# A hybrid decoder block on one core: the mixers' front with double pages, early key lengths, an early fetch of the first solved block, and the solver's steps over two blocks

## The chip, the cores and the metric

One core of a Trainium2 chip runs the whole layer as one program. The metric is the device time of that core in microseconds (us), the median of several runs. TensorE is called PE (its weight loads PEld), VectorE DVE, ScalarE ACT, GpSimd POOL and the queue that issues nearly all DMAs SP.

## What is computed

512 tokens of width 1024 go through one layer: a norm, one input projection of 3328 columns whose columns feed two mixers side by side (differential attention with partial rotary, and an RWKV-7 time mix), an output projection, an expert-retrieval FFN, a gated embedding and a final norm. Only the mixers' front is touched. What matters of it:

```python
def rwkv7_mix(z_rw, mu, ...):
    zs = z_rw + (prev - z_rw) * mu          # prev: the row before
    r, k, v, xw, xa, xg = split(zs)
    w = -softplus(-(w0 + tanh(xw) @ w_up)) - 0.5
    a = sigmoid(a0 + xa @ a_up)
    kk = k * k_k;  k = k * (1.0 + (a - 1.0) * k_a)
    kk = kk / max(sqrt(sum(kk * kk per head)), 1e-12)
    # scan over the tokens, per head of 64:
    state = state * d + (state @ -kk) x (kk * a) + v x k;  y = state @ r
```

The attention side turns the first 16 of each 64 columns of q and k by a rotary angle.

## The kernel before, in words

Tokens are worked in four blocks of 128 (NB = 4). Everything is float32; a projection is three matmuls of split halves ("whi" from ACT, L130; "wlo", the rest, from DVE, L141), its weights fetched by SP in pieces of 512 KB into three buffers.

**Order.** In the mixers (`mixers`, L866 on) the order of each engine's instructions and the slots of the buffers are set by a planner at build time, which goes roughly by program order and waits where no slot is free; a few edges written by hand (`behind`) put an instruction after another one on its engine. Working buffers are pages of two sizes: `p2` (32 pages of 512 floats a partition) and `p4` (12 pages of 1024).

**The projections of the time mix.** Four groups of columns, k, l (256 columns), r and v, are projected one after the other for all four blocks (`shift_group`, L423). `consume` scales an accumulator into a page "z"; `shift` loads the rows before it by DMA into a second page "zp" and POOL makes zs = z + (zp - z) * mu in three steps (L448, L449, L451), into a third page for k, r and v.

**Preparations.** Then block by block `rw_prepare` (L470) runs in eight parts, each ended by a yield; after each of them the loop at the end of `mixers` (L942 to L951) takes steps of two other generators: `PACE[b]` steps of the solver and `WEAVE[1 + b][i]` steps of `projections` (the three projections of attention, with rotary and transposes in `da_prepare`, L764). `rw_keys` (L455) is called at the start of a block: kk = k * k_k (L459, DVE), its square (L461, ACT), the sum per head (L463, DVE), a reciprocal square root of 12 small DVE operations (`rsqrt`, L87 on), a clamp (L465), and the scaling (L467). The first part of `rw_prepare` makes sw (L491) and aa (L495) by sigmoids, a running sum of sw by matmul (pcum, L498) and four exponentials; the next two are DVE products of 128x512 (L514 to L533); then 16 transposes (ptr, L545), `diagonal` for ab and ak (L587, L591), four stores of ab to DRAM ("ad", L561), and 256 small matmuls (pg, L570).

**Solver.** `rw_solve(half)` (L595) inverts the triangular 32x32 matrices of two blocks at once: it loads both blocks' ad (sol_u, L607), then 31 steps of a product (L613) and a sum (L615) on DVE that grow with the step, then two stores to "td" (L620). Half 0 runs in the preparation of block 2 (PACE 4), half 1 after the last preparation.

**Solved blocks.** `rw_solved(b)` (L622) clears tt on POOL (L626), loads it from td in four DMAs of 128-byte pieces (L632), loads xg (L634), bhr (L636), ykr, bk and uv (L644), multiplies tt by xg (pwu, L651), evicts to wu (L652) and multiplies wu by bhr (pmt, L663). `rw_states` and `rw_out` follow; attention blocks (`da_block`) and a small projection (`ple_proj`) are mixed in.

SP executes its DMA issues in order: one that waits for an earlier transfer's landing holds all that stand behind it.

Of the kernel before, what the change touches and what calls it, by code (L numbers as in the profile page):

```python
# [8 lines left out]
F32 = mybir.dt.float32  # L9
F32R = mybir.dt.float32r  # L10
# [20 lines left out]

WEAVE = (0, (1, 1, 1, 1, 1, 1, 0, 0), (1, 1, 1, 1, 1, 1, 0, 0), (1, 1, 1, 1, 1, 1, 0, 0), (1, 1, 1, 1, 1, 1, 0, 0))
PACE = (0, 0, 4, 0)
SUMJ = 3
MARK = "r"
DAP = 4
STEPS = 4
DA0 = (1, (0,))  # L40
PLE0 = (0, 1, 2, 3, 4, 5, 6, 7)
# [8 lines left out]
def by_row(ap):  # L50

    return bass.AP(tensor=ap.tensor, offset=ap.offset, ap=[[512, 4], [2048, 32], [1, 512]])


class Kernel:
# [361 lines left out]
    def p2(self, name, shape=(128, 512), dt=F32):  # L417
        return self.pages.tile(list(shape), dt, name=name, tag="p2", bufs=32)

    def p4(self, name, shape=(128, 1024), dt=F32):  # L420
        return self.pages.tile(list(shape), dt, name=name, tag="p4", bufs=12)

    def shift_group(self, rs, alloc, g0, n):  # L423

        nc = self.nc
        zs = {}
        zt = {}
        mu = self.p2("mu")
        nc.sync.dma_start(mu[:, :n], bcast_row(self.a["rw_mu"][:, g0:g0 + n], n))

        def consume(b, ps):
            zt[b] = self.p2("z")
            self.last_z = nc.scalar.activation(zt[b][:, :n], ps, AF.Copy, scale=rs[:, b:b + 1])
            if b == NB - 1:

                for x in range(NB):
                    shift(x)

        def shift(b):
            z, zp = zt[b], self.p2("zp")  # L440

            nc.sync.dma_start(zp[1:113, :n], z[0:112, :n])
            nc.sync.dma_start(zp[113:128, :n], z[112:127, :n])
            if b == 0:
                nc.vector.memset(zp[0:1, :n], 0.0)
            else:
                nc.sync.dma_start(zp[0:1, :n], zt[b - 1][127:128, :n])
            nc.gpsimd.tensor_tensor(zp[:, :n], zp[:, :n], z[:, :n], op=OP.subtract)  # L448
            nc.gpsimd.tensor_tensor(zp[:, :n], zp[:, :n], mu[:, :n], op=OP.mult)  # L449
            o = alloc()  # L450
            nc.gpsimd.tensor_tensor(o, z[:, :n], zp[:, :n], op=OP.add)  # L451
            zs[b] = o
        return zs, consume

    def rw_keys(self, k):  # L455

        nc, sm, p2 = self.nc, self.small, self.p2
        kk = p2("kk")
        self.behind(nc.vector.tensor_mul(kk, k, self.k_k), self.last_lo)  # L459
        sq = p2("ksq")  # L460
        self.behind(nc.scalar.activation(sq, kk, AF.Square), self.last_hi)  # L461
        nr = sm.tile([128, 8], F32, name="knr")
        nc.vector.tensor_reduce(nr, sq.rearrange("p (h i) -> p h i", h=8), axis=AX.X, op=OP.add)  # L463
        nr = self.rsqrt(sm, nr, 8, "knx")
        nc.vector.tensor_scalar(nr, nr, 1e12, None, op0=OP.min)  # L465
        kk3 = kk.rearrange("p (h i) -> p h i", h=8)
        nc.vector.tensor_tensor(kk3, kk3, nr[:, :, None].to_broadcast([128, 8, 64]), op=OP.mult)  # L467
        return kk

    def rw_prepare(self, b, psum, r, k, v, kk, lx, st):  # L470

# [147 lines left out]
            dst = bass.AP(tensor=td.tensor, offset=td.offset + 32 * par, ap=[[1024, 64], [64, 16], [1, 32]])  # L619
            nc.sync.dma_start(dst, x[64 * par:64 * par + 64])  # L620

    def rw_solved(self, b, st, post, psum):  # L622

        nc = self.nc
        tt = self.p4("tt", [128, 8, 128])
        nc.gpsimd.memset(tt, 0.0)  # L626
        for c in range(4):
            q = slice(32 * c, 32 * c + 32)
# [1 line left out]
            src = bass.AP(tensor=td.tensor, offset=td.offset + (b % 2 * 32 + c * 8) * 1024,  # L630
                          ap=[[32, 32], [1024, 8], [1, 32]])
            nc.sync.dma_start(tt[q, :, 32 * c:32 * c + 32], src)  # L632
        xg = self.p4("xg", [128, 2, 512])
        nc.sync.dma_start(xg.rearrange("p x c -> p (x c)"), self.d_xg[b])  # L634
        st["bh"], st["yk"] = self.p2("bhr"), self.p2("ykr")
        nc.sync.dma_start(st["bh"], by_row(self.d_bh[b]))  # L636
        nc.sync.dma_start(st["yk"], self.d_yk[b])

        st["bk"], st["uv"] = self.p4("bk", [128, 4, 4, 64]), self.p4("uv", [128, 4, 4, 64])
# [18 lines left out]
        for c in range(4):  # L658
            q = slice(32 * c, 32 * c + 32)
            pm = psum.tile([128, 4, 96], F32, name="pmt", tag="mm")  # L660
            for h in range(8):
                m, o = h // 2, slice(64 * (h % 2), 64 * (h % 2) + 64)
                nc.tensor.matmul(pm[o, m, 0:64], wu[q, 0, h, :], st["bh"][q, h * 64:h * 64 + 64],  # L663
                                 start=True, stop=True)
            for h in range(8):
                m, o = h // 2, slice(64 * (h % 2), 64 * (h % 2) + 64)
# [94 lines left out]
            nc.gpsimd.tensor_tensor(yf, yf, g, op=OP.mult)  # L761
            nc.gpsimd.tensor_tensor(out, yf, bvf, op=OP.add)

    def da_prepare(self, b, z, zT, psum):  # L764

        nc = self.nc
        v = z.rearrange("p (g d) -> p g d", g=8)
        t1, t2 = v[:, :, 0:8], v[:, :, 8:16]
        cos = self.cos[:, b, None, :].to_broadcast([128, 8, 8])
        sin = self.sin[:, b, None, :].to_broadcast([128, 8, 8])  # L770
        m = self.small.tile([128, 4, 8, 8], F32, name="ropem")
        nc.vector.tensor_tensor(m[:, 0], t1, cos, op=OP.mult)
        nc.vector.tensor_tensor(m[:, 1], t2, sin, op=OP.mult)
        nc.vector.tensor_tensor(m[:, 2], t2, cos, op=OP.mult)
        nc.vector.tensor_tensor(m[:, 3], t1, sin, op=OP.mult)
        nc.vector.tensor_tensor(t1, m[:, 0], m[:, 1], op=OP.subtract)
        nc.vector.tensor_tensor(t2, m[:, 2], m[:, 3], op=OP.add)
# [88 lines left out]
    def mixers(self, ocat_pool, psum):  # L866

        tc, nc, a = self.tc, self.nc, self.a
        w = a["w_in"]
        with ExitStack() as ctx:  # L870
# [33 lines left out]
            p2, p4 = self.p2, self.p4  # L904
            zs = {}
# [4 lines left out]
            for tag, c0, n in (("k", 512, 512), ("l", 1536, 256), ("r", 0, 512), ("v", 1024, 512)):  # L910
                z, consume = self.shift_group(rs, (lambda: self.small.tile([128, 256], F32, name="zsl", bufs=NB))
                                              if tag == "l" else (lambda: p2("zs")), c0, n)
                self.proj(psum, hi, lo, w, RW0 + c0, n, consume, g=g, among={} if zs else begin)
                zs[tag] = z
                if tag == MARK:
                    self.mark = self.last_hi
            self.rope_tables(cpool, cpool)
            self.lambdas(cpool)
            zd, qT, kT, vs = {}, {}, [[p4(f"kT{x}{i}", [128, 2, T], F32R) for i in range(2)]
                                  for x in ("hi", "lo")], {}  # L920

            def eat_z(b, ps):
                zd[b] = p2("z")
                nc.scalar.activation(zd[b], ps, AF.Copy, scale=rs[:, b:b + 1])

            def eat_v(b, ps):
                vs[b] = p2("dav")
# [4 lines left out]
            def projections():  # L932
                for i, eat in enumerate((eat_z, eat_z, eat_v)):
                    yield from self.proj_steps(psum, hi, lo, w, 512 * i, 512, eat, g=g)
                    for b in range(NB) if i < 2 else ():
                        if i == 0:
                            qT[b] = [p2(f"qT{x}", [128, 4, 128], F32R) for x in ("hi", "lo")]
                        self.da_prepare(b, zd[b], kT if i else qT[b], psum)
                        if b % DAP == DAP - 1:
                            yield  # L940

# [2 lines left out]
                next(ahead, None)  # L944
            for b in range(NB):
                for i, _ in enumerate(self.rw_prepare(b, psum, zs["r"][b], zs["k"][b], zs["v"][b],
                                                      self.rw_keys(zs["k"][b]), zs["l"][b], sts[b])):
                    for _ in range(PACE[b]):
                        next(solve, None)
                    for _ in range(WEAVE[1 + b][i % len(WEAVE[1 + b])]):  # L950
                        next(ahead, None)  # L951
            for _ in ahead:
# [7 lines left out]
            def rw():  # L960
                s = None
                for b in range(NB):
                    self.rw_solved(b, sts[b], post, psum)
                    yield
                    yield from self.rw_states(b, sts[b], s, psum)
                    s = sts[b]["after"]
                    self.rw_out(b, sts[b], psum, ocat[b][:, 512:1024])
                    yield
# [694 lines left out]
```

## Time and profile before

| | |
|---|---|
| runs | 1818.08, 1818.44, 1814.80 us; median 1818.08 |
| profiled execution | 1816.83 us, its span 1815.1 us |
| mean granted TensorE clock | 0.961 |
| busy share of the span | PE 94%, PEld 80%, DVE 78%, ACT 42%, POOL 35% |
| mixers (projections to the last time-mix output) | some 405 us from the start |

The profiled execution has 1.73 us outside its span, and lies 1.25 us under the median. Times in the rows below are us from the span's start. A row of the timeline has its start, its duration, engine, line, operation, output and input tile, and in brackets how long the engine stood idle before it and for whom. A tile's buffer number is left out: ps3 is shown as ps.

### The profile page before, as it was taken

What the parts mean: (1) busy time and instruction counts of PE and PEld (TensorE: products, weight loads), DVE (VectorE), ACT (ScalarE), POOL (GpSimd) and SP (SyncE); (2) the same over time, 40 slices, a digit from 0 to 9 for tenths busy, and PEclk for the clock granted to TensorE, in tenths of its full rate; (3) what the DMA queues carried; (4) which work ended last, traced back from release to release, by engine and by line L of the source; (5) the groups of instructions that cost most, each with busy time, mean ns of one, the idle gap of its engine ahead of it and who ended that gap; (6) DMA issues with size and microseconds to landing.
All of it is one profiled execution on the core that took longest, in us unless ns stands there. A gap on an engine that the chain in (4) does not pass through costs nothing.

```text
span 1815.1 us, 31087 instructions
## 1 busy us (share of the span) xinstructions
PE 1705.5 (94%) x11642; PEld 1454.9 (80%) x11642; DVE 1413.8 (78%) x3177; ACT 755.0 (42%) x1390; POOL 634.4 (35%) x548
## 2 busy tenths in 40 slices
PE   7888988899989879999999999999999999999998
PEld 6665666767777878997777888888989999998986
DVE  5357947774499998887888787878878787888885
ACT  5354532433356565444444333333333333333353
POOL 2660020213167661001111233334555555545430
PEclk9998976889999889999999999999999999999999
DMA  7453263424512433446666677788989898989891
GB/s 235 139 141 99 73 150 88 97 51 151 174 59 82 130 112 129 139 145 220 207 206 203 203 254 262 234 268 291 317 301 314 307 313 300 316 302 319 304 333 50
DMA packets 150428, 363.87 MB, mean 200 GB/s; under 512 B 43923, under 2 KB 58511, under 8 KB 150149
## 3 DMA queue, kind: packets, MB, share of 16 engines
q1 hardware_dynamic: 113412, 227.65, 38.7%
q0 software_dynamic: 36864, 134.23, 21.8%
q8 instruction: 91, 1.49, 0.3%
q14 instruction: 61, 0.49, 0.1%
HBM read 332.61 MB, written 21.36 MB: 195 GB/s over the span
## 4 chain that ended last, share of the span: by engine, by line
PE 61%; DVE 23%; ACT 4%; issue 2%; DMA 1%; SPq 0%; POOL 0%; DVEq 0%; ACTq 0%
PE po L1333 21%; PE phid L1197 8%; PE phid L1199 8%; PE phid L1198 8%; PE pg L1302 2%; DVE wlo L139 2%; ACT whi L130 2%; DVE cand L1117 2%; DVE ids L1146 1%; DVE rest L1036 1%; DVE jj L1290 1%; DVE sol_p L613 1%; DVE si L1034 1%; DVE si L1038 1%; DVE oh L1136 1%
## 5 line engine op out<-in xcount | busy, mean ns | idle before, releaser
L139 DVE TENSOR_TENSOR wlo<-wraw,whi 128x1024 fp32r<-128x1024 f32 x243 | 297.7, 1225 | 151.8 <-ACT whi L130 151.7
L1197 PE MATMUL phid<-u2dhi,whi 128*128 128x384 f32 x1024 | 351.4, 343 | 11.6 <-ACT whi L130 10.6
L130 ACT ACTIVATE whi<-wraw 128x1024 fp32r<-128x1024 f32 x276 | 291.0, 1056 | 171.1 <-PE phid L1198 59.3
L1199 PE MATMUL phid<-u2dhi,wlo 128*128 128x384 f32 x1024 | 348.7, 341 | 3.6 <-POOL wlo L139 3.6
L1198 PE MATMUL phid<-u2dlo,whi 128*128 128x384 f32 x1024 | 347.6, 339 | 0.0
L1356 POOL DMA_INDIRECT row<-in_peer_u_dram,idx x128 | 189.7, 1482 | 399.4 <-DVE row L1368 219.2
L1356 POOL DMA_INDIRECT row<-in_peer_v_dram,idx x128 | 185.6, 1450 | 276.8 <-DVE h L1372 193.7
L1333 PE MATMUL po<-whi,clo 128*128 128x512 f32 x768 | 243.2, 398 | 1.4
L1333 PE MATMUL po<-whi,chi 128*128 128x512 f32 x768 | 243.3, 398 | 1.2 <-ACT row L1206 1.2
L1333 PE MATMUL po<-wlo,chi 128*128 128x512 f32 x768 | 241.4, 395 | 0.0
L1197 PEld LDWEIGHTS phid<-u2dhi,whi 128*128 128x128 f32 x1024 | 195.3, 191 | 17.9 <-ACT whi L130 12.4
L1199 PEld LDWEIGHTS phid<-u2dhi,wlo 128*128 128x128 f32 x1024 | 194.9, 190 | 5.2 <-POOL wlo L139 5.2
L1198 PEld LDWEIGHTS phid<-u2dlo,whi 128*128 128x128 f32 x1024 | 195.1, 190 | 3.7
L1333 PEld LDWEIGHTS po<-whi,clo 128*128 128x128 f32 x768 | 143.1, 188 | 41.9 <-DVE clo L141 8.7
L1333 PEld LDWEIGHTS po<-wlo,chi 128*128 128x128 f32 x768 | 144.4, 188 | 33.6
L130 ACT ACTIVATE chi<-gelu 128x384 fp32r<-128x384 f32 x128 | 67.4, 526 | 241.4 <-DVE gelu L1310 121.7
L1372 DVE SCALAR_TENSOR_TENSOR h<-row,ids,h 128x1024 f32<-128x1024 f32 x128 | 163.9, 1280 | 1.5
L1333 PEld LDWEIGHTS po<-whi,chi 128*128 128x128 f32 x768 | 140.9, 188 | 25.6 <-ACT row L1206 1.5
L1368 DVE SCALAR_TENSOR_TENSOR row<-row,xn 128x1024 f32<-128x1024 f32 x128 | 153.6, 1218 | 0.0
L1206 ACT ACTIVATE gelu<-phid 128x384 f32<-128x384 f32 x86 | 42.2, 491 | 266.2 <-PE phid L1199 247.7
L139 POOL TENSOR_TENSOR wlo<-wraw,whi 128x256 fp32r<-128x256 f32 x132 | 96.5, 767 | 125.6 <-ACT whi L130 125.6
L208 PE MATMUL acc<-whi,uhi 128*128 128x512 f32 (+1 forms) x224 | 87.7, 399 | 18.2 <-ACT whi L130 9.6
(452 smaller groups left out, 2869.5 us busy)
## 6 DMA issues: line engine op xcount, KB each, us to landing
wraw<-in_peer_uT_dram SPq DMA_DIRECT2D x128, 512.0 KB
wraw<-in_peer_v_dram SPq DMA_DIRECT2D x128, 512.0 KB
wraw<-in_w_in_dram SPq DMA_DIRECT2D x24, 512.0 KB
wraw<-in_peer_w_q_dram SPq DMA_DIRECT2D x16, 512.0 KB
ahead<-row SPq DMA_DIRECT2D x42, 192.0 KB
gelu<-ahead SPq DMA_DIRECT2D x42, 192.0 KB
wraw<-in_w_out_dram SPq DMA_DIRECT2D x8, 512.0 KB
zp<-z SPq DMA_DIRECT2D x12, 224.0 KB
```

Source lines behind the costliest of these rows:

```text
L130: self.last_hi = nc.scalar.activation(hi, src, AF.Copy, **({} if g is None else {"scale": g}))
L139: self.last_lo = eng.tensor_tensor(lo[s], src[s], hi[s].bitcast(F32), op=OP.subtract)
L208: nc.tensor.matmul(o, hi[:, k, s], whi, start=(k == 0), stop=False)
L1117: nc.vector.tensor_tensor(cand[:, :, at:at + ni * nj].rearrange("p h (i j) -> p h i j", j=nj), sv[:, :, 0, i:i + ni, None].to_broadcast(sh ...
L1197: nc.tensor.matmul(ps, whi[:, s], hi[:, k, :], start=(k == 0), stop=False)
L1198: nc.tensor.matmul(ps, whi[:, s], lo[:, k, :], start=False, stop=False)
L1199: nc.tensor.matmul(ps, wlo[:, s], hi[:, k, :], start=False, stop=(k == KC - 1))
L1206: nc.scalar.activation(g, ps, AF.Gelu)
L1333: nc.tensor.matmul(outs[b, e], lhs[:, s], rhs[:, 512 * e:512 * e + 512], start=(c == 0 and rhs is vhi and lhs is chi), stop=(c == NKEY - 1 ...
L1356: nc.gpsimd.indirect_dma_start(out=row, out_offset=None, in_=a["peer_u" if kind == "U" else "peer_v"], in_offset=bass.IndirectOffsetOnAxis ...
L1368: nc.vector.scalar_tensor_tensor(row, row, 1.0, xn0, op0=OP.mult, op1=OP.mult, accum_out=hid0[:, k:k + 1])
L1372: nc.vector.scalar_tensor_tensor(acc0, row, hid0[:, k:k + 1], acc0, op0=OP.mult, op1=OP.add)
```

## The change

Seven edits, all in `mixers` and the functions that it calls.

- `shift_group`: z and zp become the two halves of one tile: a p4 page where the group has 512 columns (k, r, v), a p2 page for l.
- `rw_keys` takes all four blocks, is called once, ahead of the projection of group v, and computes one reciprocal square root over 32 columns.
- Rotary works on two blocks at once (`da_rope`), its temporaries in a p2 page; two blocks' attention z share one p4 page.
- The pages of kT are taken after the projection of the attention's keys rather than before the preparations.
- `PACE` is (0, 0, 3, 2): 24 solver steps in block 2, the last 7 and the store in parts 0 to 3 of block 3.
- `rw_fetch` (clear tt, load tt and xg) is split from `rw_solved`; for block 0 it is issued after part 4 of block 3 (`FETCH0`). bhr of block 0 is loaded after part 0 of block 3 (`FETCH1`), into a p4 page. For the other blocks both stand where they stood.
- `WEAVE[1]` begins with 2, 2: block 0 takes 8 steps of `projections` instead of 6, and all 26 steps are taken by the end of block 3.

```diff
-WEAVE = (0, (1, 1, 1, 1, 1, 1, 0, 0), (1, 1, 1, 1, 1, 1, 0, 0), (1, 1, 1, 1, 1, 1, 0, 0), (1, 1, 1, 1, 1, 1, 0, 0))
-PACE = (0, 0, 4, 0)
+WEAVE = (0, (2, 2, 1, 1, 1, 1, 0, 0), (1, 1, 1, 1, 1, 1, 0, 0), (1, 1, 1, 1, 1, 1, 0, 0), (1, 1, 1, 1, 1, 1, 0, 0))
+PACE = (0, 0, 3, 2)
+FETCH0 = (3, 4)
+FETCH1 = (3, 0)
...
-            zt[b] = self.p2("z")
+            if n == 256:
+                zz[b] = self.p2("zz", [128, 2, 256])
+            else:
+                zz[b] = self.p4("zz", [128, 2, 512])
+            zt[b] = zz[b][:, 0]
...
-            z, zp = zt[b], self.p2("zp")
+            z, zp = zt[b], zz[b][:, 1]
...
+        nr = sm.tile([128, NB * 8], F32, name="knr", bufs=1)
+        kks = []
+        for b in range(NB):
+            kk = p2("kk")
+            self.behind(nc.vector.tensor_mul(kk, ks[b], self.k_k), self.last_lo)
+            sq = p2("ksq")
+            self.behind(nc.scalar.activation(sq, kk, AF.Square), self.last_hi)
+            nc.vector.tensor_reduce(nr[:, b * 8:b * 8 + 8], sq.rearrange("p (h i) -> p h i", h=8), axis=AX.X, op=OP.add)
+            kks.append(kk)
+        nr = self.rsqrt(sm, nr, NB * 8, "knx")
         nc.vector.tensor_scalar(nr, nr, 1e12, None, op0=OP.min)
-        kk3 = kk.rearrange("p (h i) -> p h i", h=8)
-        nc.vector.tensor_tensor(kk3, kk3, nr[:, :, None].to_broadcast([128, 8, 64]), op=OP.mult)
-        return kk
+        for b, kk in enumerate(kks):
+            kk3 = kk.rearrange("p (h i) -> p h i", h=8)
+            nc.vector.tensor_tensor(kk3, kk3, nr[:, b * 8:b * 8 + 8, None].to_broadcast([128, 8, 64]), op=OP.mult)
+        return kks
...
+    def rw_fetch(self, b, st):
+        nc = self.nc
+        st["tt"], st["xg"] = tt, xg = self.p4("tt", [128, 8, 128]), self.p4("xg", [128, 2, 512])
         nc.gpsimd.memset(tt, 0.0)
...
+    def rw_fetch_bh(self, b, st):
+        st["bh"] = self.p4("bhr", [128, 512]) if b == 0 else self.p2("bhr")
+        self.nc.sync.dma_start(st["bh"], by_row(self.d_bh[b]))
...
+    def da_rope(self, z, b):
+        v = z.rearrange("p b (g d) -> p b g d", g=8)
+        t1, t2 = v[:, :, :, 0:8], v[:, :, :, 8:16]
+        cos, sin = (x[:, b:b + 2, None, :].to_broadcast([128, 2, 8, 8]) for x in (self.cos, self.sin))
+        m = self.p2("rope", [128, 4, 2, 8, 8])
...
+                if tag == "v":
+                    kk = self.rw_keys(zs["k"])
                 self.proj(psum, hi, lo, w, RW0 + c0, n, consume, g=g, among={} if zs else begin)
...
+                    if (b, i) == FETCH0:
+                        self.rw_fetch(0, sts[0])
+                    if (b, i) == FETCH1:
+                        self.rw_fetch_bh(0, sts[0])
...
                 for b in range(NB):
+                    if b:
+                        self.rw_fetch(b, sts[b])
                     self.rw_solved(b, sts[b], post, psum)
```

## Rows read from the trace of the kernel before

**Rows 1.** Busy time by stretch of the front; the first line names the columns.

```profile
core 0: us, PE busy (x) PEld busy (x) DVE busy (x) ACT busy (x) POOL busy (x), PEclk, DMA share, GB/s
66.00:102.00 36.00, 31.22 (x128) 24.83 (x127) 10.90 (x13) 12.92 (x25) 24.24 (x24) 0.95 0.44 128
102.00:126.00 24.00, 24.00 (x102) 18.68 (x101) 13.52 (x18) 11.57 (x17) 15.67 (x11) 1.00 0.51 140
126.00:149.00 23.00, 13.74 (x296) 10.08 (x294) 18.44 (x39) 11.24 (x18) 3.83 (x3) 0.78 0.49 135
149.00:179.00 30.00, 25.07 (x350) 18.10 (x349) 21.96 (x67) 15.48 (x27) 0.00 (x0) 0.94 0.25 74
179.00:212.00 33.00, 28.82 (x370) 21.15 (x369) 30.66 (x113) 18.58 (x33) 0.86 (x4) 1.00 0.30 85
212.00:242.00 30.00, 27.99 (x178) 20.44 (x178) 29.81 (x58) 13.95 (x22) 6.42 (x7) 0.95 0.35 93
242.00:263.00 21.00, 15.03 (x234) 11.19 (x236) 3.27 (x15) 6.24 (x10) 5.75 (x11) 0.67 0.86 202
263.00:280.00 17.00, 16.42 (x159) 12.63 (x163) 6.20 (x29) 3.21 (x13) 0.00 (x0) 0.50 0.29 55
280.00:320.00 40.00, 34.42 (x383) 26.23 (x383) 32.52 (x107) 12.15 (x35) 3.57 (x3) 0.74 0.34 98
```

**Rows 2.** Timeline, PE: two waits of the preparations, and the first solved block.

```profile
104.22 1.02 PE L489 MATMUL plw<-w_up,lw 65*128 65x512 f32 x2
...
138.80 1.09 PE L545 MATMUL ptr<-ident,be 128*128 128x128 f32 x4 [6.98 <-DVE be L524]
...
257.91 3.75 PE L651 MATMUL pwu<-xg,tt 128*128 128x128 f32 x16 [2.93 <-DMA xg<-d_xg]
262.92 0.69 PE L663 MATMUL pmt<-bhr,wu 32*64 32x64 f32 x8 [1.26 <-DMA bhr<-d_bh]
```

**Rows 3.** Timeline, ACT: block 0's first sigmoid, block 3's last eviction.

```profile
128.41 0.60 ACT L491 ACTIVATE sw<-plw 128x512 f32<-128x512 f32 x1
...
246.75 0.60 ACT L572 ACTIVATE akv<-pg 128x512 f32<-128x512 f32 x1 [0.25 <-PE pg L570]
```

**Rows 4.** Timeline, DVE: keys of block 0, solver's last seven steps, a short operation.

```profile
38.86 0.17 DVE L376 TENSOR_SCALAR x0q<-x0q 128x32 f32<-128x32 f32 x1
...
39.05 1.31 DVE L376 TENSOR_SCALAR h1q<-h1q 128x32 f32<-128x32 f32 x1
...
125.75 0.68 DVE L459 TENSOR_TENSOR kk<-zs,b_rw_k_k 128x512 f32<-128x512 f32 x1
...
132.86 0.68 DVE L500 SCALAR_TENSOR_TENSOR e_ex<-sw,pcum 128x512 f32<-128x512 f32 x1
...
213.89 0.75 DVE L613 TENSOR_TENSOR sol_p<-sol_x,sol_u 128x338 f32<-128x338 f32 x1
...
230.36 0.71 DVE L615 TENSOR_REDUCE sol_x<-sol_p 128x16 f32<-128x512 f32 x1
```

**Rows 5.** Groups of DVE instructions, 126 to 242 us: busy, mean ns, idle before.

```profile
L467 DVE TENSOR_TENSOR kk<-kk,knx 128x512 f32<-128x512 f32 x4 | 2.8, 692 | 0.1
...
L463 DVE TENSOR_REDUCE knr<-ksq 128x8 f32<-128x512 f32 x4 | 2.7, 686 | 8.0 <-ACT ksq L461 8.0
...
L776 DVE TENSOR_TENSOR z<-ropem 128x64 f32<-128x64 f32 x8 | 1.7, 216 | 0.0
```

**Rows 6.** Timeline, SP: issues of DMAs around the last preparation.

```profile
231.13 1.31 SPq L620 DMA_DIRECT2D td<-sol_x  x2
...
250.96 1.14 SPq L607 DMA_DIRECT2D sol_u<-ad  x2
252.19 2.01 SPq L632 DMA_DIRECT2D tt<-td  x4
254.30 0.39 SPq L634 DMA_DIRECT2D xg<-d_xg  x1
```

**Rows 7.** The chain that ended last, 225 to 300 us: start, duration.

```profile
245.75 5.08 DMA ad<-ab
```

More of the change, by code (lines that the diff above doesn't have):

```diff
@@ L426, in shift_group @@
         zs = {}
-        zt = {}
+        zt, zz = {}, {}
         mu = self.p2("mu")
@@ L453, in shift_group, with rw_keys @@
         return zs, consume
-    def rw_keys(self, k):
+    def rw_keys(self, ks):
         nc, sm, p2 = self.nc, self.small, self.p2
[L458 to L464, printed above, removed]
+        nr = sm.tile([128, NB * 8], F32, name="knr", bufs=1)
[8 more added lines that the diff above has]
+        nr = self.rsqrt(sm, nr, NB * 8, "knx")
         nc.vector.tensor_scalar(nr, nr, 1e12, None, op0=OP.min)
-        kk3 = kk.rearrange("p (h i) -> p h i", h=8)
-        nc.vector.tensor_tensor(kk3, kk3, nr[:, :, None].to_broadcast([128, 8, 64]), op=OP.mult)
-        return kk
+        for b, kk in enumerate(kks):
+            kk3 = kk.rearrange("p (h i) -> p h i", h=8)
+            nc.vector.tensor_tensor(kk3, kk3, nr[:, b * 8:b * 8 + 8, None].to_broadcast([128, 8, 64]), op=OP.mult)
+        return kks
     def rw_prepare(self, b, psum, r, k, v, kk, lx, st):
@@ L620, in rw_solve @@
             nc.sync.dma_start(dst, x[64 * par:64 * par + 64])
-    def rw_solved(self, b, st, post, psum):
+    def rw_fetch(self, b, st):
         nc = self.nc
-        tt = self.p4("tt", [128, 8, 128])
+        st["tt"], st["xg"] = tt, xg = self.p4("tt", [128, 8, 128]), self.p4("xg", [128, 2, 512])
         nc.gpsimd.memset(tt, 0.0)
@@ L632, in rw_solved @@
             nc.sync.dma_start(tt[q, :, 32 * c:32 * c + 32], src)
-        xg = self.p4("xg", [128, 2, 512])
         nc.sync.dma_start(xg.rearrange("p x c -> p (x c)"), self.d_xg[b])
-        st["bh"], st["yk"] = self.p2("bhr"), self.p2("ykr")
-        nc.sync.dma_start(st["bh"], by_row(self.d_bh[b]))
+    def rw_fetch_bh(self, b, st):
+        st["bh"] = self.p4("bhr", [128, 512]) if b == 0 else self.p2("bhr")
+        self.nc.sync.dma_start(st["bh"], by_row(self.d_bh[b]))
+    def rw_solved(self, b, st, post, psum):
+        nc = self.nc
+        tt, xg = st["tt"], st["xg"]
+        if "bh" not in st:
+            self.rw_fetch_bh(b, st)
+        st["yk"] = self.p2("ykr")
         nc.sync.dma_start(st["yk"], self.d_yk[b])
@@ L762, in rw_out, with da_turn @@
             nc.gpsimd.tensor_tensor(out, yf, bvf, op=OP.add)
-    def da_prepare(self, b, z, zT, psum):
+    def da_rope(self, z, b):
         nc = self.nc
[L767 to L777, printed above, removed]
+        v = z.rearrange("p b (g d) -> p b g d", g=8)
+        t1, t2 = v[:, :, :, 0:8], v[:, :, :, 8:16]
+        cos, sin = (x[:, b:b + 2, None, :].to_broadcast([128, 2, 8, 8]) for x in (self.cos, self.sin))
+        m = self.p2("rope", [128, 4, 2, 8, 8])
+        m = [m[:, i] for i in range(4)]
+        nc.vector.tensor_tensor(m[0], t1, cos, op=OP.mult)
+        nc.vector.tensor_tensor(m[1], t2, sin, op=OP.mult)
+        nc.vector.tensor_tensor(m[2], t2, cos, op=OP.mult)
+        nc.vector.tensor_tensor(m[3], t1, sin, op=OP.mult)
+        nc.vector.tensor_tensor(t1, m[0], m[1], op=OP.subtract)
+        nc.vector.tensor_tensor(t2, m[2], m[3], op=OP.add)
+    def da_turn(self, z, zT, psum, b):
+        nc = self.nc
         pt = psum.tile([128, 4, 128], F32, name="ptq", tag="tp")
@@ L918, in mixers @@
             self.lambdas(cpool)
-            zd, qT, kT, vs = {}, {}, [[p4(f"kT{x}{i}", [128, 2, T], F32R) for i in range(2)]
-                                  for x in ("hi", "lo")], {}
+            zd, qT, kT, vs = {}, {}, [], {}
             def eat_z(b, ps):
-                zd[b] = p2("z")
-                nc.scalar.activation(zd[b], ps, AF.Copy, scale=rs[:, b:b + 1])
+                if b % 2 == 0:
+                    zd[b // 2] = p4("z", [128, 2, 512])
+                nc.scalar.activation(zd[b // 2][:, b % 2], ps, AF.Copy, scale=rs[:, b:b + 1])
             def eat_v(b, ps):
@@ L934, in projections @@
                     yield from self.proj_steps(psum, hi, lo, w, 512 * i, 512, eat, g=g)
+                    if i == 1:
+                        kT.extend([p4(f"kT{x}{j}", [128, 2, T], F32R) for j in range(2)] for x in ("hi", "lo"))
                     for b in range(NB) if i < 2 else ():
@@ L937, in projections @@
                             qT[b] = [p2(f"qT{x}", [128, 4, 128], F32R) for x in ("hi", "lo")]
-                        self.da_prepare(b, zd[b], kT if i else qT[b], psum)
+                        if b % 2 == 0:
+                            self.da_rope(zd[b // 2], b)
+                        self.da_turn(zd[b // 2][:, b % 2], kT if i else qT[b], psum, b)
                         if b % DAP == DAP - 1:
@@ L946, in mixers @@
                 for i, _ in enumerate(self.rw_prepare(b, psum, zs["r"][b], zs["k"][b], zs["v"][b],
-                                                      self.rw_keys(zs["k"][b]), zs["l"][b], sts[b])):
+                                                      kk[b], zs["l"][b], sts[b])):
                     for _ in range(PACE[b]):
                         next(solve, None)
+                    if (b, i) == FETCH0:
+                        self.rw_fetch(0, sts[0])
+                    if (b, i) == FETCH1:
+                        self.rw_fetch_bh(0, sts[0])
                     for _ in range(WEAVE[1 + b][i % len(WEAVE[1 + b])]):
```

## The prediction

> **What bounds the kernel now.** I read first the busy times by stretch [rows 1], to see which engine limits which part of the front, then the timelines of PE and ACT at the two places where PE stands [rows 2, 3], then DVE's [rows 4, 5], and SP's queue with the chain of waits for the solved block [rows 6, 7]. All times are of the profiled execution: 1816.83 us, of which 1815.1 are its span; the median of the runs is 1.25 us above it, and I add that at the end. After the front (some 405 us) nothing is edited, so whatever the front gives or loses moves the rest with it, one for one.
>
> Five places matter in the front. From 66 to 102 us PE is nearly full while DVE is busy 10.90 of 36 us [rows 1]. From 102 to 126 PE is full with a projection of attention, though the inputs of block 0's preparation are there: its first matmul ran at 104.22 [rows 2], and the sigmoid that reads it runs only at 128.41 [rows 3]. Between them stand the keys: the product at 125.75, then squares, sums, the square root, until e_ex at 132.86 [rows 4]. PE waits 6.98 us for DVE at 138.80 [rows 2]. So the stretch from 126 to 149 holds PE work of only 13.74 us at a clock of 0.78, some 10.7 at full clock [rows 1]. From 149 to 179 PE is busy 25.07 of 30 us, and DVE waits, over the whole 116 us, 8.0 us for the squares [rows 1, 5]. From 179 to 242 DVE is busy 60.5 of 63 us and PE 56.8 [rows 1]: here the solver's 62 instructions come on top of two preparations. Last, block 3's final eviction ends at 247.35 [rows 3], but the product that opens the solved block starts at 257.91 [rows 2]. SP explains it: it first waits for block 3's ab to land (5.08 us [rows 7]), issues sol_u at 250.96, and only then tt and xg [rows 6], though td had been stored since 231.13. After that stand come 17 us in which PE is full at a clock of 0.50, the lower of its two levels (1.2 of 2.4 GHz), where 242 to 263 had a mean of 0.67 [rows 1].
>
> **The change, part by part.** Keys in the projections. Four blocks have 12 instructions of 0.68 to 0.69 us (product, sum, scaling [rows 4, 5]), 8.2 us, and one chain of 13 short ones instead of four. They stand on DVE ahead of the weight splits of group v, and PE waits for those. DVE has 36 less 10.90, that is 25.1 us free there [rows 1]. A short instruction takes 0.17 us, or 1.31 when it is held [rows 4], so the 25 instructions cost 10.4 us at best and 32.8 at worst. The mean of the 13 DVE instructions of that stretch is 0.84 us [rows 1], which makes 21 us: under 25.1, covered, so I take 0. The ends are 0 and +8 (32.8 less 25.1). The four squares go on ACT behind the last split of r; ACT is busy 12.92 of 36 us and the next split waits behind them; taken as covered.
>
> That worst case has a known reason. The Trainium skill (SBUF — State Buffer, "SBUF: two separate sides") says that VectorE and GpSimd take a shared pair of ports as an exclusive lock, and that the loser blocks until the other's instruction is done. The 1.31 beside 0.17 [rows 4] agrees. By the rule alone the keys would cost the +8, since POOL is busy 24.24 of the 36 us there; it is a rival below.
>
> Double pages. z and zp leave the small pages for idle large ones: per 512-column group 8 small pages less. Whether a missing page or the planner's order kept the keys at 125.75 no row tells. With the keys gone and pages free, block 0's sigmoids can follow 104.22. **Block 0:** the chain from 125.75 to 132.86, 7.1 us, disappears; the most is 23 less 10.7, that is 12.3, if the preparation runs wholly beside the projection before it (two more steps of it are woven in there), and the least 2, if DVE is merely replaced by sigmoid and exponentials. I take 7, PE's own idle row of 6.98.
>
> **Block 1:** no more wait for squares, and two scalings less. PE's idle 4.9 us of the 30 and its clock of 0.94 limit this to 6; least 0. I take 3.
>
> **Blocks 2 and 3:** DVE, nearly full, loses 2 x 2.06 = 4.1 us of keys, and of 26 short ones about half their 4.4 (they overlap others), 2.2. Rotary of k has 24 instructions of 0.216 [rows 5], 5.2 us, against 12 of double size, between 2.6 and 5.2; I take 3.8, a gain of 1.4. Sum 7.7, but PE has only 6.2 us of idle to give. I take 5, ends 0 and 6.2. PACE itself only moves steps inside this stretch.
>
> Front up to the gap: 0 + 7 + 3 + 5 = **15 us**, ends -6 (the keys' 8 less block 0's least 2) and 24.5.
>
> **The early fetch.** The last seven solver steps are 14 instructions, 0.75 and 0.71 us the first and the last [rows 4], some 10.2 us, and now stand among block 3's own work. The solver's end therefore moves from 231.07 to somewhere before 242, where DVE's full stretch ends; I take 238, nearer the late end. Then two stores, 1.31 [rows 6], and their landing, not shown; the nearest is ad's 5.08 [rows 7]: 244.4. SP waits for that, then issues tt (2.01) and xg (0.39): 246.9. xg's issue ended at 254.69 and the product began at 257.91, so 3.2 us more: 250.1 on the old clock, 7.8 before 257.91. Ends: 3.8, if the solver ends at 242, and 10.6, if the operands are there at 247.35. bhr, loaded a part of a block earlier, no longer costs its 1.26 [rows 2]. Together **9 us**.
>
> What queues behind the new wait: SP is held from about 239 to 244.4, then for tt and xg, and block 3's stores of ab, the load of sol_u, and bk and uv stand behind. They come some 4.5 us later against the rest. The solver's second half is not needed until block 2, and the first product and pmt need none of these; I take 0, at most 4.5.
>
> **The clock.** If the stand goes, the 16.42 us of PE at 0.50 [rows 1] could be 8.2. Nothing shows that it will be granted; ends 0 and 8.2, I take 4. **Given back:** from 280 to 320 DVE is busy 32.52 and PE 34.42 of 40 us [rows 1], so 13 us of shift in the solved chain meet work that doesn't shrink. Ends 0 and 9; I take 4.
>
> Sum: 15 + 9 + 4 - 4 = **24 us** less, 1792.8 in the profiled execution, **1794** on the median.
>
> **Rivals.** (a) **Pages run out, slower.** Four kk pages live from the projections to their block. With r, k and v of four blocks that is 16, with the rotated q 24; one preparation takes about 16 more, and there are 32. If a block's first page then comes free only with the last store of the block before it, blocks no longer overlap. It decides where a block's first sigmoid waits for the former block's last eviction to be stored. The price of such a start is seen in 126 to 149: 23 us for 10.7 of PE work, 12.3. Two blocks lose 24.6 and the 8 of blocks 1 to 3 don't come; 7 + 9 stay: +9, 1827. For it: the chain already waits at that place. Against: z, zp and attention's z leave the small pages.
>
> (b) **The keys' price.** If each instruction meets POOL, +8, and block 0's 7 go too, since the weights of v come late: 24 - 15 = 9 us less, 1809. The Trainium skill's rule named above would give this one. Against it: DVE's mean of 0.84 in the same stretch.
>
> (c) **The head start is not used.** If block 0 gains only its least 2, blocks 2 and 3 nothing, and the solved chain waits for bk and uv, which SP issues later, only some 4 us remain: 1814.
>
> **How the numbers follow.** The main case, 24 less, has 0.68; (a) 0.10; (b) 0.10; (c) 0.12, which lies on the line of 0.2% (3.6 us, about what a measurement of this kernel can tell) and is split 0.05 faster and 0.07 same. So faster 0.83, same 0.07, slower 0.10. The low end takes block 0's 12.3, blocks 1 to 3 at 12.2, the fetch's 11.9, a clock of 4 and nothing given back, 40 us: 1778. The high end, 1817, takes in (b) and (c) and leaves (a) and the far low corner out, about 2 in 10.
>
> **What would show it.** Right: the key lengths lie before 102 us and DVE has no wait for squares after it; block 0's sigmoid stands well before 128; PE's 6.98 is gone; tt's loads stand ahead of ad's stores on SP, and pwu follows the last eviction within 3 us; the stretch after it has a clock above 0.50; out of 405 some 20 us are missing. Wrong: PE idle for wlo near 79 to 90 us (b); idle at each block's first sigmoid (a); pwu early, but the states at the same distance from the end (c); or td's loads landing after 255, which would mean that the solver's end moved past block 3.

## The result and the profile after

The changed kernel takes 1804.04 us at the median of 8 runs (1800.8 to 1806.73); the kernel before, beside it, 1816.91 (8 runs, 1812.86 to 1825.53). The ratio is 0.9928, 95% interval 0.9910 to 0.9945: 13 us or 0.7% faster. The profiled execution has 1806.73 us, a span of 1805.0 and a mean granted clock of 0.967, 10.1 us less than the one before; it is the slowest of the eight. In what follows b0 to b3 are the four blocks.

Busy time by stretch, the changed kernel, in the stretches and columns of [rows 1], with the first 66 us added:

```profile
0.00:66.00 66.00, 45.64 (x218) 38.94 (x219) 37.24 (x84) 26.90 (x44) 26.39 (x48) 0.95 0.58 181
66.00:102.00 36.00, 36.00 (x156) 29.02 (x155) 20.04 (x22) 16.01 (x29) 21.01 (x19) 1.00 0.57 176
102.00:126.00 24.00, 18.77 (x62) 13.12 (x61) 19.64 (x35) 13.51 (x20) 17.24 (x13) 0.79 0.42 119
126.00:149.00 23.00, 22.81 (x348) 17.44 (x347) 15.52 (x27) 13.55 (x24) 3.95 (x3) 1.00 0.48 146
149.00:179.00 30.00, 29.80 (x316) 22.36 (x320) 20.05 (x43) 13.83 (x23) 0.00 (x0) 1.00 0.33 96
179.00:212.00 33.00, 31.29 (x456) 22.59 (x446) 24.41 (x80) 19.48 (x34) 0.86 (x4) 1.00 0.41 116
212.00:242.00 30.00, 22.19 (x243) 17.40 (x245) 28.75 (x47) 13.53 (x22) 13.55 (x13) 0.86 0.37 127
242.00:263.00 21.00, 14.52 (x264) 12.97 (x258) 3.87 (x20) 4.72 (x12) 0.93 (x4) 0.74 0.73 150
263.00:280.00 17.00, 16.44 (x164) 12.19 (x163) 9.56 (x40) 3.68 (x15) 0.00 (x0) 0.76 0.18 56
```

Four things are to be seen. From 126 to 212 us PE is now busy 83.9 of 86 us at full clock, where [rows 1] has 67.6. From 212 to 242 it has lost work, 22.19 for 27.99, while DVE is nearly as full as it was. The solver's last seven steps stand there in both kernels, to 231.07 before and to 240.69 now. After 263 the clock is 0.76, not 0.50. And the first 66 us, which nobody looked at before, hold 45.64 us of PE; the kernel before had

```profile
0.00:66.00 66.00, 52.06 (x253) 43.25 (x254) 34.17 (x90) 30.66 (x48) 23.87 (x44) 0.97 0.67 212
```

PE's and ACT's timelines, the changed kernel, at the places of [rows 2, 3]:

```profile
125.01 0.60 ACT L501 ACTIVATE sw<-plw 128x512 f32<-128x512 f32 x1
136.39 0.60 PE L555 MATMUL ptr<-ident,be 128*128 128x128 f32 x4
234.72 2.41 ACT L954 ACTIVATE dav<-acc,r_mix 128x512 f32<-128x512 f32 x4
238.07 1.86 PE L597 MATMUL psA<-art,ktT 64*32 64x64 f32 x64 [4.83 <-DVE ab L601]
244.48 0.60 ACT L582 ACTIVATE akv<-pg 128x512 f32<-128x512 f32 x1 [0.60 <-PE pg L580]
253.15 3.75 PE L670 MATMUL pwu<-xg,tt 128*128 128x128 f32 x16 [5.83 <-DMA tt<-td]
```

b0's sigmoid comes 3.4 us earlier than in [rows 3], and PE's 6.98 us of waiting at ptr [rows 2] is gone. The attention's last projection is read (dav) at 234.7, at 247.24 before. But b3's last eviction (akv) is only 2.3 us earlier, and PE still waits for the solved block: pwu comes 8.1 us after akv's end, 10.6 before. pwu gains 4.8 us in all.

SP's queue, DVE's last solver step, and the chain of waits around it (answering to [rows 4, 6, 7]):

```profile
240.01 0.68 DVE L625 TENSOR_REDUCE sol_x<-sol_p 128x16 f32<-128x512 f32 x1
240.95 5.84 SPq L630 DMA_DIRECT2D td<-sol_x  x2
249.87 1.80 SPq L642 DMA_DIRECT2D tt<-td  x4
251.77 1.12 SPq L617 DMA_DIRECT2D sol_u<-ad  x2
...
242.52 7.27 DMA td<-sol_x
```

tt's load stands ahead of sol_u now, as written. What it waits for is no longer SP's place but the data: the solver ends at 240.69 (231.07 before), its store takes 7.27 us to land, and only then tt can be read.

By milestones (start, before and after): v's accumulators of the time mix 101.05, 104.22 (+3.2); last akv 246.75, 244.48 (-2.3); pwu 257.91, 253.15 (-4.8); pmt 262.92, 256.82 (-6.1); pwu of b1 313.29, 304.15 (-9.1); the first addition after the output projection 430.36, 423.94 (-6.4); end of the span 1815.1, 1805.0 (-10.1).

### The profile page after: what moved, and what is told of

Same layout as the page of the kernel before. It is cut to its first block, busy times and chain, and to the rows that moved or that the text cites. A ratio compares the mean times of both kernels' runs of the same rounds, so it can differ in the third digit from the quotient of the medians.

```text
span 1805.0 us, 31001 instructions
## 1 busy us (share of the span) xinstructions
PE 1695.9 (94%) x11642; PEld 1449.4 (80%) x11642; DVE 1417.5 (79%) x3114; ACT 754.4 (42%) x1390; POOL 638.5 (35%) x548
## 4 chain that ended last, share of the span: by engine, by line
PE 68%; DVE 24%; ACT 4%; issue 2%; DMA 1%; SPq 0%; POOL 0%; DVEq 0%; ACTq 0%
PE po L1369 21%; PE phid L1233 9%; PE phid L1235 9%; PE phid L1234 9%; PE pg L1338 2%; DVE wlo L141 2%; PE acc L210 2%; PE acc L211 2%; PE acc L212 2%; ACT whi L132 2%; DVE cand L1153 1%; DVE ids L1182 1%; DVE sol_p L623 1%; DVE rest L1072 1%; DVE jj L1326 1%
## 5 line engine op out<-in xcount | busy, mean ns | idle before, releaser
L211 PE MATMUL acc<-wlo,uhi 128*128 128x512 f32 (+1 forms) x224 | 89.8, 401 | 10.7 <-DVE wlo L143 10.7
```

Of the source, the lines that this page charges most:

```text
L211: nc.tensor.matmul(o, hi[:, k, s], wlo, start=False, stop=False)
```

## The experiments

Eleven more kernels, and the changed one again (e12), ran in three groups, each against the kernel before on the same chip (medians there: 1816.69 of 30 runs, 1815.99 of 17, 1814.44 of 24). Executions of one kernel spread by 3 to 16 us, so verdicts rest on medians and intervals, and a single profile only says where things stand. Differences to the changed kernel are taken to its median of 1804.04; e12 gave 1805.72, so each of them is uncertain by 2 us and more.

**e1, solver back in block 2.**

```diff
-PACE = (0, 0, 3, 2)
+PACE = (0, 0, 4, 0)
```

> The changed kernel with PACE back to (0, 0, 4, 0): all 31 solver steps in the preparation of block 2, the early fetch kept. Theory A: the split only makes the solver end late (240.7 us in the changed kernel, and its DVE time falls into block 3, where DVE is full while it has slack in block 2), so td lands late and the early fetch is half spent. Then the solver's last sum ends before 232 us, the first product of tt and xg follows the last eviction of block 3 within 3 us (8.1 in the changed kernel), and the time falls by 4 to 8 us, to 1796 to 1800. Rival B: the split is what frees block 3's preparation; with it undone, block 2's stores of ab and block 3's first sigmoid come 3 us or more later, and the time rises by 2 to 6 us.

1809.85 us (12 runs), ratio 0.9955 [0.9937, 0.9973]: 5.8 us slower than with the split. ACT, SP and PE in it:

```profile
235.52 1.60 SPq L630 DMA_DIRECT2D td<-sol_x  x2
244.60 2.84 ACT L954 ACTIVATE dav<-acc,r_mix 128x512 f32<-128x512 f32 x4 [12.94 <-PE acc L212]
248.28 1.07 ACT L582 ACTIVATE akv<-pg 128x512 f32<-128x512 f32 x2
248.97 2.02 PE L670 MATMUL pwu<-xg,tt 128*128 128x128 f32 x16 [0.40 <-ACT akv L582]
```

td is stored 5.4 us earlier, pwu follows akv at once and comes 4.2 us earlier than in the changed kernel. For that, dav comes 10 us later and akv ends 4.3 later. DVE and PE in e1, and then PE in the changed kernel:

```profile
237.80 1.40 DVE L143 SCALAR_TENSOR_TENSOR wlo<-wraw,g_mix,whi 128x512 fp32r<-128x512 f32 x2
237.69 0.89 PE L597 MATMUL psA<-art,ktT 64*32 64x64 f32 x28 [5.61 <-DVE ab L601]
272.91 1.91 PE L726 MATMUL plg<-g_up,lg 128*128 128x512 f32 x2
```

```profile
270.39 1.37 PE L726 MATMUL plg<-g_up,lg 128*128 128x512 f32 x2
```

The last two weight splits (wlo) of the attention's projection now stand on DVE behind the solver, at 237.80; in the changed kernel the last one is at 218.35. So that projection ends later, and PE's work that the changed kernel has done before pwu (attention's psS and six accr) follows it here: plg, a product behind the solved block, begins 2.5 us later although pwu began 4.2 earlier. The time is rival B's; its sign is nearly there (b3's first sigmoid 2.5 us later, not 3). Theory A's solver end before 232 did not come either (235.42). PE's wait for ab at psA is as long as in the changed kernel, so the split doesn't make it.

**e2, no early fetch.**

```diff
-FETCH0 = (3, 4)
-FETCH1 = (3, 0)
+FETCH0 = FETCH1 = None
...
-                    if b:
-                        self.rw_fetch(b, sts[b])
+                    self.rw_fetch(b, sts[b])
```

> The changed kernel without the early fetch: tt, xg and bhr of block 0 are loaded where they were before the change, the solver still over two blocks. Theory A: the fetch is worth the 4.8 us by which the first product came earlier: it goes back behind the load of sol_u and that of ab, and the time rises by 3 to 7 us, to 1807 to 1811. Rival B: td lands so late that the loads wait at the same place anyway; the time stays within 2 us of 1804.

1811.59 us (12 runs), ratio 0.9976 [0.9957, 0.9994]: 7.5 us are lost, theory A and 0.6 us beyond its range. The profile (its fastest execution) has two waits back, those of [rows 2]:

```profile
256.05 3.75 PE L669 MATMUL pwu<-xg,tt 128*128 128x128 f32 x16 [6.38 <-DMA xg<-d_xg]
260.96 0.45 PE L681 MATMUL pmt<-bhr,wu 32*64 32x64 f32 x8 [1.16 <-DMA bhr<-d_bh]
```

They show 2.9 us at pwu and 4.1 at pmt; the rest of the 7.5 that profile does not show.

**e3, keys block by block.**

```diff
-                if tag == "v":
-                    kk = self.rw_keys(zs["k"])
...
-                                                      kk[b], zs["l"][b], sts[b])):
+                                                      self.rw_keys(zs["k"][b]), zs["l"][b], sts[b])):
```

> The changed kernel with the key lengths computed per block in the preparation again. Theory A: the keys in the preparations cost a chain of short operations ahead of each block's second part; undone, block 0's second product stage starts 3 to 5 us later and the time rises by 4 to 8 us, to 1808 to 1812, although v's accumulators are emptied up to 2 us earlier. Rival B: what the keys cost beside POOL's shifts (1.78 us for a product of 0.68) is as much as they save; the time stays within 2 us of 1804.

1803.59 us (7 runs), ratio 0.9929 [0.9904, 0.9954]: the same as with the keys early, rival B. b0's sigmoid even comes sooner:

```profile
120.82 0.60 ACT L497 ACTIVATE sw<-plw 128x512 f32<-128x512 f32 x1
```

The step behind the keys, e_ex of b0, starts at 128.33, in the changed kernel at 128.07. So the keys' move is not what freed block 0.

**e4, small pages for z and the rows before.**

```diff
-            if n == 256:
-                zz[b] = self.p2("zz", [128, 2, 256])
-            else:
-                zz[b] = self.p4("zz", [128, 2, 512])
-            zt[b] = zz[b][:, 0]
+            zt[b] = self.p2("z")
...
-            z, zp = zt[b], zz[b][:, 1]
+            z, zp = zt[b], self.p2("zp")
```

> The changed kernel with z and zp in two small pages again, as before the change. Theory A: the double pages only let the planner place the loads of the row before ahead of the next group's weights on SP, so that PE stands 5.5 and 5.2 us in group l; undone, group l's accumulators are emptied some 10 us earlier, group v's 2 to 3, and the time is 1800 to 1804. Rival B: the small pages are needed by the preparations; undone, block 0's first sigmoid comes 5 us or more later and the time rises by 4 to 10 us.

1812.04 us (12 runs), ratio 0.9971 [0.9952, 0.9990]: 8 us lost, rival B. SP and POOL in it, at v's shifts:

```profile
116.09 0.60 SPq L481 DMA_DIRECT2D d_v<-zs  x1
123.93 0.38 SPq L167 DMA_DIRECT2D wraw<-in_w_in_dram  x1
124.36 0.53 SPq L444 DMA_DIRECT2D zp<-z  x1
130.56 1.80 POOL L450 TENSOR_TENSOR zp<-zp,z 128x512 f32<-128x512 f32 x1 [9.86 <-DMA zp<-z]
131.68 0.60 ACT L497 ACTIVATE sw<-plw 128x512 f32<-128x512 f32 x1
```

The load of the third block's zp is issued only after a store of v and behind a weight fetch at 123.93; POOL waits 9.86 us for its data. With large pages all of v's loads are out by 115.7. That a small page came free late is the likely reason, but no row names it.

**e8, both of these undone.** The two diffs above together.

> As after, but with the keys block by block and with small pages for z and the rows before, both as in before. Theory A (small pages alone lose 8 us only because the keys made early hold four small pages through v's projection and block 0; with keys per block small pages are as good): 1803 to 1806 us, v's accumulators at 101 to 103, sw of block 0 at 121 to 128. Rival B (the larger pages are themselves the gain, for the small ones run out in the attention's projections too): 1809 to 1813 us, sw of block 0 at 128 or later.

1810.45 us (12 runs), ratio 0.9975 [0.9958, 0.9992]. Rival B: small pages lose some 6 us with late keys too, so the four early key pages are not the reason.

**e5, k's shifts later.** `loads` are the loads of a block's rows before it, `shift_k` the shift function of group k.

```diff
-            if b == NB - 1:
+            if b == NB - 1 and g0 != 512:
...
+            for x in loads if g0 == 512 else ():
+                self.behind(x, self.fetches[-1])
...
+                begin = {0: [lambda x=x: shift_k(x) for x in range(NB)]} if tag == "l" else {}
```

> As after, but group k's rows before it are loaded, and its three POOL steps made, in the first part of r's projection, behind r's first weight fetch, instead of right after k's accumulators. Theory A (the larger pages let the planner issue all eleven zz loads ahead of l's weights, and POOL's sixteen us of shifts then stretch the rotary table's DVE steps to 1.26 us; that is the +10 us at l's accumulators, and +3.2 is left of it at v's): the two stalls of PE in l (5.54 and 5.20 us) shrink to under 3 us together, l's accumulators are read at 48 to 51 instead of 58.95, v's at 100 to 102 instead of 104.2, and the end moves with them: 1800 to 1802 us median. Rival B (r and v are bound by weights, l's loss was made good anyway, what is left at v's comes from the keys beside POOL): l's at 50 but v's stay at 103.5 to 104.5, 1803.5 to 1805 us.

1802.02 us (6 runs), ratio 0.9929 [0.9907, 0.9950]. What it was to cure, PE in group l of the changed kernel, and then the same in e5:

```profile
46.21 0.58 PE L211 MATMUL acc<-wlo,uhi 128*128 128x256 f32 x1 [5.54 <-DVE wlo L143]
56.20 0.58 PE L211 MATMUL acc<-wlo,uhi 128*128 128x256 f32 x1 [5.20 <-DVE wlo L143]
```

```profile
56.31 1.55 SPq L167 DMA_DIRECT2D wraw<-in_w_in_dram  x3
61.48 0.79 PE L210 MATMUL acc<-whi,uhi 128*128 128x512 f32 x1 [9.93 <-ACT whi L132]
```

l's accumulators were read at 44.93 instead of 58.95, but the wait went to r's second weights, which SP issues at 56.31 behind the 22 loads of k's and l's rows. v's accumulators gained 1.1 us. Theory A's mechanism holds only for l; the stand was moved, not removed. The median lies at the edge of its range, 2 us under the changed kernel's, which the spread of either alone can make.

**e6, k's shifts later and keys block by block.** The diffs of e5 and e3 together.

> As the kernel with k's shifts later, and the keys made block by block again. Theory A: both savings add, sw of block 0 at 117 to 119 (after 125.0, keys per block alone 120.8), the front's end 5 to 7 us before after's, 1797 to 1800 us median. Rival B (an earlier start is taken by the solver's half in blocks 2 and 3, which fills DVE from 212 on): sw of block 0 earlier, the attention's last dav and the first pwu within 2 us of the kernel with keys per block alone (232.3, 251.9), 1802 to 1804 us.

1802.26 us (6 runs), ratio 0.9922 [0.9898, 0.9945]. Rival B in time, pwu and dav: pwu at 253.38, dav at 232.79, no better than either alone. b0's sigmoid, at 120.94, is not earlier than with the keys per block alone (120.82).

**e7, six steps in block 0.**

```diff
-WEAVE = (0, (2, 2, 1, 1, 1, 1, 0, 0), ...
+WEAVE = (0, (1, 1, 1, 1, 1, 1, 0, 0), ...
```

> As after, but block 0 takes 6 steps of the attention's projections again, not 8, so two are left for after the last block. Theory A (the two steps bring the attention's v forward, dav 247.2 to 234.7, and with it the stretch between preparations and first solved block): dav of block 3 back behind 243, first pwu 2 to 4 us later, 1806 to 1808 us. Rival B (the steps fill time of PE that is idle after the last block anyway, where PE waits for td): dav later, but pwu within 1 us of 253.15, and 1803 to 1805 us.

1802.73 us (6 runs), ratio 0.9927 [0.9907, 0.9947]. Nearer to rival B, 0.3 us under its range: dav is back at 243.77, yet pwu comes 3.3 us earlier than in the changed kernel (1.7 us earlier than in e12, at 251.52).

```profile
249.81 2.94 PE L670 MATMUL pwu<-xg,tt 128*128 128x128 f32 x16 [1.64 <-DMA tt<-td]
```

The two steps that are left over lie where PE would wait for td.

**e9, the pages alone; e10, the split and the fetch alone.** e9 is the changed kernel with e1's, e2's, e3's and e7's edits; e10 with those of e3, e4 and e7. Rotary on two blocks and late kT pages stand in both.

> Before, with the larger pages for z and the rows before it, the rotary on two blocks and the late kT pages, and none of the rest: keys block by block, the solver in block 2, no early fetch, six steps in block 0. Theory A (the parts hold each other up: larger pages move the preparations forward, but without the solver's split and the early fetch the first solved block waits for td all the same, so alone they bring a third of the 13 us): 1811 to 1814 us. Rival B (they are worth the 8 us that taking them away costs, whatever stands beside them): 1807 to 1809.5 us. Rival C (without the split they bring nothing): 1815 to 1817 us.

> Before, with the solver's steps over two blocks and the early fetch (and the rotary on two blocks), but small pages, keys block by block and six steps in block 0. Theory A (block 0 starts late behind v's shifts, and the early fetch then gains as much as beside the larger pages): 1809 to 1812 us, as with only keys and pages undone (1810.45), for the two steps of block 0 are worth nothing. Rival B (the two steps are what the small pages lacked): over 1813 or under 1808 us.

e9: 1815.23 us (12 runs), ratio 0.9990 [0.9971, 1.0009], its theory C. e10: 1814.48 us (12 runs), ratio 0.9989 [0.9972, 1.0006], its rival B: it is 4 us slower than e8, from which it differs by the two steps of block 0 alone, though the two intervals overlap. Neither half by itself can be told from no change. PE at the solved block, e9 (its slowest execution):

```profile
263.22 3.60 PE L665 MATMUL pwu<-xg,tt 128*128 128x128 f32 x16 [3.59 <-DMA xg<-d_xg]
```

and e10, with ACT's read of the attention's last projection:

```profile
252.06 2.79 ACT L944 ACTIVATE dav<-acc,r_mix 128x512 f32<-128x512 f32 x4 [1.44 <-PE acc L212]
253.72 0.40 PE L212 MATMUL acc<-whi,ulo 128*128 128x512 f32 x1
254.81 2.00 PE L662 MATMUL pwu<-xg,tt 128*128 128x128 f32 x16
278.19 1.91 PE L718 MATMUL plg<-g_up,lg 128*128 128x512 f32 x2
```

In e9 the wait for the loads of [rows 2] is still there. In e10 pwu waits for nothing, tt is in time; but the attention's projection keeps PE until 254.1. pwu is 3.1 us earlier than before, and yet plg starts at 278.19, where it started before (278.05): as in e1, the work that the projection held up follows pwu.

**e11, k's shifts later and six steps in block 0; e12, the changed kernel once more.** The diffs of e5 and e7 together; e12 has no edit.

> As after, with k's shifts in r's projection and block 0 with six steps of the attention's projections. Theory A (l's stalls go, and the two steps left for the end fill PE's wait for td): 1799 to 1801.5 us median. Rival B (each alone moved the median by no more than the executions differ, and both together do no better): 1801.5 to 1804 us.

> The changed kernel again, beside the others of this group, so that they stand against it on the same chip: 1802 to 1806 us by all theories. If the spread between executions alone explains the differences of 1 to 2 us seen so far, its median lies within 2 us of 1804.04 on either side.

e11: 1798.23 us (6 runs, 1796.63 to 1803.86), ratio 0.9914 [0.9889, 0.9939]; e12: 1805.72 us (7 runs, 1800.96 to 1806.99), ratio 0.9947 [0.9923, 0.9971]. e11 lies just under theory A's range and is the best kernel here, 7.5 us under the changed one beside it, though the intervals of the two ratios overlap; four of its six runs lie under the fastest of the changed kernel's fifteen. ACT and PE in it:

```profile
239.23 2.42 ACT L958 ACTIVATE dav<-acc,r_mix 128x512 f32<-128x512 f32 x4
245.39 3.53 PE L671 MATMUL pwu<-xg,tt 128*128 128x128 f32 x16 [0.36 <-DMA tt<-td]
```

Blocks 0 to 2 start 5 to 6 us earlier than in the changed kernel (b0 at 119.30), the leftover steps fill the wait, and 5.83 us of it (2.96 in e12) become 0.36.

## Why the prediction was right, and where its steps failed

Direction and range held: forecast 24 us less, measured 13 (10.1 between the profiled executions), inside the range. The sum was too large by eleven, and its parts were off by more. By the milestones, the 10.1 us are 2.3 up to akv (15 forecast), 3.8 more up to pmt (9), 0.3 more to the output projection (0), and 3.7 behind that, where the forecast had nothing. That the total still lies in the range, 39 us wide, is partly luck: what was lost in group l (3.2 us left at v's) and what was gained behind the front (3.7) were both unforeseen, and cancel.

**Keys in the projections, 0.** Wrong as to place and as to price. The products lie at 92.0 to 102.4, three of the four beside POOL, but the chain and the scaling end at 112.3, not before 102:

```profile
92.04 3.48 DVE L468 TENSOR_TENSOR kk<-zs,b_rw_k_k 128x512 f32<-128x512 f32 x2
98.34 0.68 DVE L468 TENSOR_TENSOR kk<-zs,b_rw_k_k 128x512 f32<-128x512 f32 x1
100.64 1.78 DVE L468 TENSOR_TENSOR kk<-zs,b_rw_k_k 128x512 f32<-128x512 f32 x1
109.81 2.50 DVE L477 TENSOR_TENSOR kk<-kk,knx 128x512 f32<-128x512 f32 x4
112.23 0.41 DVE L495 COPY lw<-ptl 64x256 f32<-64x256 f32 x1
112.69 2.08 PE L499 MATMUL plw<-w_up,lw 65*128 65x512 f32 x2 [5.23 <-DVE lw L495]
```

Rival (b) had the mechanism for the products: 1.78 us beside POOL for the 0.68 of [rows 4]. The sums were not held (two took 1.26 us together at 97.15, beside POOL). From 66 to 102 this cost PE nothing, 36.00 of 36 us. The price came behind that stretch, where the sum did not look: a copy that b0's first product needs stands on DVE behind the scalings, and PE waits 5.23 us for it. Every kernel with early keys has this wait (3.36 to 5.23 us), and e3 has none; e3 pays 2.83 us at ptr and 2.14 at pcum in its place. So the whole move is worth nothing either way, but the 0 is a price of 5 us against a gain, not a covered cost.

**Block 0, 7.** Its reason failed: "With the keys gone and pages free, block 0's sigmoids can follow 104.22". e3 keeps the keys in the block and starts b0's sigmoid earlier still, e4 keeps them out and starts it at 131.68. It is the pages. They keep v's loads together on SP (e4's rows), and that was the case the prediction left open, "no row tells". In size, e_ex came at 128.07 for 132.86, 4.8 us. Rival (a) did not come with the change (b1's sigmoid waits 0.17 us).

**Front up to the gap, 15: the step that failed.** PE's side of it came: dav 12.5 us earlier, PE full from 126 to 212. The preparations' side did not. Their e_ex starts 4.8 us earlier in b0, but 0.2 later in b1 and 0.7 later in b2, 5.0 earlier in b3, and the last akv is 2.3 earlier. The fault is to take the idle time of PE and DVE in each block as that block's gain, 7 + 3 + 5. PE's idle time was filled with the attention's projections, and from then on the preparations wait for PE. DVE in the changed kernel, at b2:

```profile
184.33 0.69 DVE L510 SCALAR_TENSOR_TENSOR e_ex<-sw,pcum 128x512 f32<-128x512 f32 x1 [6.57 <-PE pcum L508]
```

With two projection steps fewer in b0 (e7), b1's sigmoid comes at 147.75 for 150.00 and b2's at 179.86 for 182.10. So b0's head start is gone by b1, before the solver begins. The solver needs b1's ab; it begins at 189.55 (187.02 before), has 8.58 us of DVE from 179 to 212 (13.85 before) and 17.90 from 212 to 242 (11.47 before). There it meets b3's preparation, DVE is busy 28.75 of 30 us, and PE waits 4.83 us for ab at psA (1.40 before). "PACE itself only moves steps inside this stretch" held for the place of the steps, and the split does not make that wait: e1 has 10.00 and 15.63 us of solver there, and waits 5.61. What PACE also moves is the weight splits beside the steps (e1's wlo), which the sum put at nothing; by e1 it is worth 5.8 us. Why the solver gets less of DVE before 212 is open. The outcome is rival (c)'s in part, by another cause than its bk and uv.

**The early fetch, 9.** Mis-sized in two terms: the solver ended at 240.69, not 238, and its stores were down 9.1 us after that, not 6.4, the second one taking 7.27 us to land for ad's 5.08. From there to pwu it was 3.4 us, not 5.6, which gave 2 of the 5 back. So pwu stands 8.1 us behind akv where the forecast had 3. bhr's 1.26 came. By e2 the fetch is worth 7.5 us of the median, more than the 4.1 that its profile shows at pmt.

**The clock, 4, and given back, 4.** The sizes fit: from -6.1 at pmt to -9.1 at b1's pwu, then back to -6.4 at the output projection. That the clock made the 3 us is not shown: it is 0.76 for 0.50 from 263 to 280, but 0.70 for 0.74 from 280 to 320, and e12, the same kernel, has 0.93 and 0.62. "One for one" after the front was not: the gain grows from 6.4 to 10.1 by the end, part of it where PE begins the next projection:

```profile
455.00:475.00 20.00, 16.64 (x69) 13.07 (x70) 6.43 (x10) 4.33 (x7) 0.00 (x0) 0.91 0.92 289
```

In the kernel before that stretch had a clock of 0.83.

**The unforeseen loss.** In group l the larger pages let the planner issue all eleven loads of k's rows ahead of l's weights; POOL's shifts then stretch the rotary tables' short operations, and the last wlo stands behind them. l's accumulators came 10 us later, of which 3.2 are left at v's. e5 shows that the loss does not vanish by order alone.

**The parts are not a sum.** Taken away one at a time, the pages cost 8, the fetch 7.5, the split 5.8, together 21 for a change of 13; alone on the kernel before, the pages and the split with the fetch bring 2 or less each (ratios 0.9990 and 0.9989). The rows at pwu show why: it needs both PE done with the projections and tt in place. e10 has the second without the first, e2 the first without the second. And after pwu PE is full (16.44 of 17 us from 263 to 280), so an early pwu with PE's other work still to do, as in e1 and e10, brings nothing at plg. That e9's later blocks fall behind (b2's sigmoid at 186.61, 181.09 before) was seen in its slowest execution only, and its cause is open. Rotary on two blocks and the late kT pages were not tried by themselves; alone with the pages (e9) they bring nothing that can be told.

## What to carry to other kernels

Where a start has two conditions, find both last arrivals before pricing either: an edit that serves one of them is worth nothing alone, and undoing parts one by one will count the gain twice. Idle time that an edit frees goes to whatever stands next on that engine, not to the work that one had in mind, so ask what that is. A step that is moved in the program's order need not move in time: look where it ran before and after, and what moved beside it. Larger buffers change the order of a shared queue as well as its waits, so read the queue at the places that the edit was not meant for.

## What the runs showed of the hardware

DVE was held by POOL instruction by instruction. POOL and DVE in the kernel before, where the short operation takes 0.17 us alone [rows 4]:

```profile
40.40 1.34 POOL L449 TENSOR_TENSOR zp<-zp,mu 128x512 f32<-128x512 f32 x1
40.48 1.31 DVE L378 SCALAR_TENSOR_TENSOR h1y<-h1q,h1y 128x32 f32<-128x32 f32 x1
```

The short one lasts as long as POOL's. The lock that the Trainium skill describes (SBUF — State Buffer, "SBUF: two separate sides") agrees with this pair, and with the keys' 1.78 for 0.68.

A store of 128 KB in 128-byte pieces (td) needed 7.27 us from issue to landing, and what reads it back waits for all of that; in the six other runs whose chain of waits shows this store it was 4.94 to 7.56 us. And two executions of the same changed kernel differ in the wait at pwu by half (5.83 and, in e12, 2.96 us), so that a profile of one execution does not price a few us here.
